# A feed-forward block with seven block products per tile pair, and its output product in one pass over all PSUM banks

## The chip, the cores and the metric

The kernel runs on one core of one Trainium2 chip. The metric is device time in microseconds (us). The kernel before was run three times: median 1025.72 us, 1024.86 to 1025.85 us.

## The reference

One layer of a hybrid encoder on 512 tokens of 1024 channels, in fp32: RMSNorm, one combined projection into three token mixers, a gated merge, an output projection with a residual, and then the feed-forward part, which alone is changed here, and a last RMSNorm:

```
h2 = rmsnorm(x, ffn_norm_g)                              # x: [512 tokens, 1024]
gate, up = jnp.split(h2 @ w_ffn_in, 2, axis=-1)          # each [512, 2816]
x = x + (jax.nn.silu(gate) * up) @ w_ffn_out             # [512, 1024]
out = rmsnorm(x, final_norm_g)
```

## The kernel before

**Operands.** Every large product is formed from fp32 operands that are each split into two float32r parts: a high part (a cast, `hi`) and a low part (`lo = raw - hi`). `mm3` (lines 162 to 165) issues three matmuls for one 128-deep slice: high by high, high by low, low by high. A weight tile of 128 by 1024 is loaded by one 512 KB DMA into one of three buffers (tag `w`, `load_raw`), cast on ScalarE and subtracted on VectorE (`parts`, lines 148 to 156) into two buffers of tag `wh` and two of tag `wl`.

**Feed-forward.** 2816 hidden channels are 22 tiles `m` of 128. For a tile, gate and up are each one PSUM bank [128 channels, 512 tokens], a sum over 8 slices of the 1024 input channels: 2 x 8 x 3 = 48 matmuls of 512 columns (lines 1121 to 1126). The first tile is done in two halves of 256 tokens (`ff0`, lines 1097 to 1102), so that its first half can start before the last token tiles are normed. ScalarE takes SiLU, VectorE multiplies by up, and the product is split into parts at once (lines 1127 to 1140). After every second tile, the two new hidden tiles are multiplied by the first 512 output columns of the output weights, into four banks `acc` (lines 1141 to 1144). When all 22 tiles are done, a second pass over them makes the other 512 output columns (lines 1152 to 1163), token tile after token tile at the end; the last token tile is in two pieces of 256 columns.

**Order.** Instructions are issued by a scheduler that takes them by priority (trace order, with weight loads and their splits raised by `HP`), when a buffer is free in its model. On the chip each engine works its queue in order.

**Around it.** `residual` (line 1080) adds the input to the output projection, norms and transposes a token tile; `norm_B` (line 226) moves it from PSUM into the parts `h2`. The last loop (lines 1159 to 1176) does residual, RMSNorm and the store. V, A, G, T stand for VectorE, ScalarE, GpSimd and TensorE; `cs(k)` is the k-th slice of 128 columns, `U`, `DD`, `TT`, `XT_` take buffers of the pools `up`, `dp`, `tp`, `xp`.

Of the kernel before, what the change touches and what calls it, by code (L numbers as in the profile page):

```python
# [44 lines left out]
# estimated delays of the chains' steps, for the order in which they are traced  # L45
# [10 lines left out]
def trunk(ctx, tc, a, out, dbg=None):  # L56
# [105 lines left out]
    def mm3(ps, lh, ll, rh, rl, first, last):  # L162
        T.matmul(ps, lh, rh, start=first, stop=False)  # L163
        T.matmul(ps, lh, rl, start=False, stop=False)  # L164
        T.matmul(ps, ll, rh, start=False, stop=last)  # L165
# [34 lines left out]
    def rms_factor(xs, ss=None, eng=None):  # L200
        """xs: the halves of a token tile."""
# [887 lines left out]
    ff0 = []  # L1089
    for t in range(NT):  # L1090
# [12 lines left out]
    tap("x2", x2[0][0])  # L1103

# [1 line left out]
    acc = [SM("acc") for _ in range(NT)]  # L1106
    fw = {}
    hid = []

    def ffn_out(k, t, n, ps, c=slice(0, 512)):  # L1110
        if (k // 2, n) not in fw:
            src = a["wfo"][2 * (k // 2):2 * (k // 2) + 2, :, 512 * n:512 * n + 512].rearrange("k p c -> p k c")
            fw[k // 2, n] = load_w(src)
        wh, wl = fw[k // 2, n]
        hh, hl = hid[k]
        r = slice(512 * (k % 2) + c.start, 512 * (k % 2) + c.stop)
        mm3(ps[:, c], hh[:, cs(t)], hl[:, cs(t)], wh[:, r], wl[:, r], k == 0, k == FT - 1)

    for m in range(FT):
        pr = ff0 if m == 0 else []  # L1120
        for g in range(2 if m else 0):
            wh, wl = load_w(a["wfi"][2 * m + g])
            ps = BIG("ff")
            for k in range(KT):
                mm3(ps, wh[:, cs(k)], wl[:, cs(k)], h2.hi(k), h2.lo(k), k == 0, k == KT - 1)
            pr.append(ps)
        s = TT("silu")
        last = A.activation(s, pr[0], AF.Silu)
        V.tensor_tensor(s, s, pr[1], op=ALU.mult)  # L1129
        if m < 4:  # L1130
            ho = op.tile([P, 2, S], F32R, tag="o", name=nm("ho"))
            hh, hl = ho[:, 0], ho[:, 1]
        elif m < 8:
            tg = ("toe", "pt", "sc", "kq")[m - 4]
            hh, hl = XT_("hh", tg, F32R), XT_("hl", tg, F32R)
        else:
            hh, hl = (DD if m < 8 + ND else UU)("hh", F32R)
        A.copy(hh, s)
        V.tensor_tensor(hl, s, hh.bitcast(F32), op=ALU.subtract)
        hid.append((hh, hl))  # L1140
        if m % 2 == 1:
            for k in (m - 1, m):
                for t in range(NT):
                    ffn_out(k, t, 0, acc[t])
# [7 lines left out]
    KF = 18
    pieces = [[(slice(0, 512), BIG("acc2"))] for _ in range(NT - 1)]
    pieces.append([(slice(0, 256), SM("acc2")), (slice(256, 512), SM("acc2"))])
    for k in range(KF):
        for t in range(NT):
            for r, ps in pieces[t]:
                ffn_out(k, t, 1, ps, r)
    for t in range(NT):
        xt, xg = x2[t], TT("xg")  # L1160
        for i, (r, ps) in enumerate(pieces[t]):
            for k in range(KF, FT):
                ffn_out(k, t, 1, ps, r)
            V.tensor_tensor(xt[1][:, r], ps[:, r], xt[1][:, r], op=ALU.add)
            if i < len(pieces[t]) - 1:
                sq_sum(xt[1][:, r], ss[t][:, 1:2])
                V.tensor_tensor(ss[t][:, 0:1], ss[t][:, 0:1], ss[t][:, 1:2], op=ALU.add)
            (V if t == NT - 1 else G).tensor_tensor(xg[:, r], xt[1][:, r], gb[:, 512 + r.start:512 + r.stop], op=ALU.mult)
        G.tensor_tensor(xt[0], xt[0], gb[:, 0:512], op=ALU.mult)  # L1169
        rs = rms_factor([None, xt[1][:, r]], ss[t])  # L1170
        for n, y in enumerate((xt[0], xg)):
            if n == 0 and t < NT - 1:
# [6 lines left out]
def pack(i):  # L1179
    """Lays the inputs out for the loads; no arithmetic."""  # L1180
# [84 lines left out]
```

## Time and profile before

| | |
|---|---|
| three runs | 1025.85, 1025.72, 1024.86 us (median 1025.72) |
| profiled execution | span 1025.0 us from first to last instruction; no other time of it is given |
| TensorE | busy 1005.8 us (98%), 5388 matmuls |
| VectorE / ScalarE / GpSimd | busy 529.8 (52%) / 443.4 (43%) / 139.3 us (14%) |
| feed-forward part | from about 655 us to the end |

Busy time of TensorE overlaps from one matmul to the next, since matmuls are pipelined: what a matmul takes in a dense stream is the distance from its start to the start of the next one. An engine's other instructions are read by their mean duration. In the slices of the page each digit is a fortieth of the span in tenths.

### The profile page before, as it was taken

Reading aid. Unit: us, or ns where it says so; the run is one execution under the profiler, and the core shown is the slowest. Engines: PE = TensorE matmul, PEld = TensorE weight load, DVE = VectorE, ACT = ScalarE, POOL = GpSimd, SP = SyncE. Lnnn points to the kernel's source line nnn. Section 1 sums busy time; section 2 is a strip of 40 time slices with the busy share of each in tenths; the row PEclk is TensorE's granted clock in tenths of the full one; section 3 lists DMA queues with packets and bytes.
Section 4 is the critical chain, followed back from the end, with each engine's and each line's share of the span. In section 5 each row is a group of like instructions: output and inputs, shape, how many; then the busy total and the mean of one; then the engine's idle time right before and its main releaser. Section 6 shows DMA issues by size and latency. Waiting matters only on the chain.

```text
span 1025.0 us, 13638 instructions
## 1 busy us (share of the span) xinstructions
PE 1005.8 (98%) x5388; PEld 820.6 (80%) x5388; DVE 529.8 (52%) x924; ACT 443.4 (43%) x715; POOL 139.3 (14%) x153
## 2 busy tenths in 40 slices
PE   6999999999999999999999999999999999999996
PEld 5777887887887877777888878988888888888885
DVE  6688845486456677766543545633333333233324
ACT  5366345254554557564453644432222222223313
POOL 5115120000223312232121220000000000000201
PEclk8999998699999999999999999999999999999998
DMA  6424271011332211122223235133223322332322
GB/s 213 166 82 123 81 207 62 22 42 63 92 103 83 82 63 62 63 83 83 74 91 103 82 103 185 63 103 103 100 85 103 103 92 94 103 101 85 103 95 90
DMA packets 33008, 98.31 MB, mean 96 GB/s; under 512 B 3504, under 2 KB 3776, under 8 KB 32944
## 3 DMA queue, kind: packets, MB, share of 16 engines
q1 hardware_dynamic: 31120, 91.14, 26.9%
q0 software_dynamic: 1824, 6.31, 2.2%
q8 instruction: 42, 0.69, 0.3%
q14 instruction: 22, 0.18, 0.1%
HBM read 91.65 MB, written 5.78 MB: 95 GB/s over the span
## 4 chain that ended last, share of the span: by engine, by line
PE 94%; DVE 3%; ACT 1%; issue 1%; DMA 1%; POOL 0%; SPq 0%; DVEq 0%; ACTq 0%; POOLq 0%
PE pj L163 11%; PE pj L165 10%; PE pj L164 10%; PE ff L165 8%; PE ff L164 8%; PE ff L163 8%; PE acc L164 4%; PE acc L163 4%; PE acc L165 4%; PE br L163 2%; PE br L165 2%; PE br L164 2%; PE ov L822 1%; PE pv L163 1%; PE pv L165 1%; PE pv L164 1%
## 5 line engine op out<-in xcount | busy, mean ns | idle before, releaser
L151 ACT CAST wh<-w 128x1024 fp32r<-128x1024 f32 x150 | 157.9, 1053 | 406.0 <-PE ff L164 163.9
L155 DVE TENSOR_TENSOR wl<-w,wh 128x1024 fp32r<-128x1024 f32 x148 | 193.9, 1310 | 258.9 <-ACT wh L151 256.4
L163 PE MATMUL pj<-hTh,wh 128*128 128x512 f32 x464 | 185.5, 400 | 0.6 <-DVE cvo L384 0.6
L165 PE MATMUL pj<-hTh,wl 128*128 128x512 f32 x464 | 185.0, 399 | 0.0
L164 PE MATMUL pj<-hTl,wh 128*128 128x512 f32 x464 | 184.6, 398 | 0.0
L163 PE MATMUL ff<-h2h,wh 128*128 128x512 f32 (+1 forms) x368 | 139.9, 380 | 0.0
L165 PE MATMUL ff<-h2h,wl 128*128 128x512 f32 (+1 forms) x368 | 139.8, 380 | 0.0
L164 PE MATMUL ff<-h2l,wh 128*128 128x512 f32 (+1 forms) x368 | 139.8, 380 | 0.0
L163 PEld LDWEIGHTS pj<-hTh,wh 128*128 128x128 f32 x464 | 87.8, 189 | 19.9 <-issue 2.2
L165 PEld LDWEIGHTS pj<-hTh,wl 128*128 128x128 f32 x464 | 88.0, 190 | 18.9 <-issue 1.6
L164 PEld LDWEIGHTS pj<-hTl,wh 128*128 128x128 f32 x464 | 88.0, 190 | 18.2 <-issue 1.3
L164 PEld LDWEIGHTS ff<-h2l,wh 128*128 128x128 f32 x368 | 69.2, 188 | 13.2
L163 PEld LDWEIGHTS ff<-h2h,wh 128*128 128x128 f32 x368 | 69.2, 188 | 13.1
L165 PEld LDWEIGHTS ff<-h2h,wl 128*128 128x128 f32 x368 | 69.2, 188 | 13.0
L164 PE MATMUL acc<-wl,hh 128*128 128x512 f32 (+1 forms) x162 | 59.5, 367 | 0.0
L163 PE MATMUL acc<-wh,hh 128*128 128x512 f32 (+1 forms) x162 | 59.2, 366 | 0.0
L1169 POOL TENSOR_TENSOR x<-x,gb 128x512 f32<-128x512 f32 x4 | 6.0, 1540 | 343.6 <-ACT sq L195 343.6
L1129 DVE TENSOR_TENSOR silu<-silu,ff 128x512 f32<-128x512 f32 x22 | 15.1, 688 | 72.2 <-PE ff L165 72.2
L165 PE MATMUL acc<-wh,hh 128*128 128x512 f32 (+1 forms) x126 | 46.0, 365 | 0.0
L163 PE MATMUL br<-oh,wh 128*128 128x512 f32 x96 | 38.2, 398 | 0.0
L165 PE MATMUL br<-oh,wl 128*128 128x512 f32 x96 | 37.7, 392 | 0.0
L1029 POOL TENSOR_TENSOR y<-y,yt 128x512 f32<-128x512 f32 x16 | 22.5, 1406 | 110.6 <-DVE yt L1028 110.6
(319 smaller groups left out, 1602.2 us busy)
## 6 DMA issues: line engine op xcount, KB each, us to landing
w<-in_wb SPq DMA_DIRECT2D x60, 512.0 KB, 3.5
w<-in_wfi SPq DMA_DIRECT2D x44, 512.0 KB, 3.5
w<-in_wfo SPq DMA_DIRECT2D x22, 512.0 KB, 3.5
w<-in_wbr SPq DMA_DIRECT2D x12, 512.0 KB, 3.5
w<-in_wv SPq DMA_DIRECT2D x8, 512.0 KB, 3.6
w<-in_wout SPq DMA_DIRECT2D x8, 512.0 KB, 3.5
x<-in_x SPq DMA_DIRECT2D x4, 512.0 KB, 7.2
toe<-in_toe SPq DMA_DIRECT2D x8, 256.0 KB, 2.9
```

Of the source, the lines that this page charges most:

```text
L151: A.copy(hi, raw)
L155: (eng or V).tensor_tensor(lo, raw, hi.bitcast(F32), op=ALU.subtract)
L163: T.matmul(ps, lh, rh, start=first, stop=False)
L164: T.matmul(ps, lh, rl, start=False, stop=False)
L165: T.matmul(ps, ll, rh, start=False, stop=last)
L822: T.matmul(po[64 * hh:64 * hh + 64, 0:P], av[kt][:, h * 64:(h + 1) * 64], PT[hh][:, cs(kt)], start=kt == 0, stop=kt == qb, tile_position=( ...
L1029: G.tensor_tensor(y[m], y[m], t, op=ALU.add)
L1129: V.tensor_tensor(s, s, pr[1], op=ALU.mult)
L1169: G.tensor_tensor(xt[0], xt[0], gb[:, 0:512], op=ALU.mult)
```

## The change

- Gate rows and up rows of a hidden tile form a block row pair, the two halves of the 1024 input channels a block column pair, and the two halves of the tokens the columns of the other factor. The 2x2 by 2x2 block product is done with seven block products instead of eight (for tiles 1 to 21; tile 0 stays as it was). One block product is 4 slices x 3 matmuls of 256 columns.
- Four sums of input blocks (`x11`, `x12`, `x22`, `x21`) are formed once from an fp32 copy `xf` of the normed tokens that `norm_B` writes besides, three on V and one on G, and split into parts. For each tile, four sums of weight blocks are formed on G, and seven weight blocks of 128 by 512 are split into parts (A casts, V subtracts), in nine rotating buffers.
- The products land in three PSUM banks of 256 columns, the three of `pb` for even tiles and three of `pq` for odd ones; A and V combine them into gate and up. Some products are added onto a bank that was read in between.
- The hidden tiles are kept in fp32 and split when the output product needs them. That product comes after all tiles: all 1024 output columns and four token tiles in eight banks at once, slice by slice for 19 of the 22, then token tile by token tile for the last three.

```diff
-    def norm_B(r, t, o):
+    def norm_B(r, t, o, xf):
...
             V.tensor_tensor(o.l[n][:, :, sl], ph, o.h[n][:, :, sl].bitcast(F32), op=ALU.subtract)
+            A.copy(xf[n][t // 2][:, :, (t % 2) * P:(t % 2) * P + P], ph)
...
+    xf = [[op.tile([P, 4, 256], F32, tag="o", name=nm("xf")) for _ in range(2)] for _ in range(2)]
...
+    def split(src, hi, lo):
+        A.copy(hi, src)
+        V.tensor_tensor(lo, src, hi.bitcast(F32), op=ALU.subtract)
+        return hi, lo
+
+    with tc.high_priority(offset=HP):
+        (x11, x12), (x21, x22) = xf
+        V.tensor_tensor(x11, x12, x11, op=ALU.subtract)
+        G.tensor_tensor(x12, x22, x12, op=ALU.subtract)
+        V.tensor_tensor(x22, x22, x11, op=ALU.subtract)
...
+        T2 = tparts(x22, "T2")
+        V.tensor_tensor(x21, x21, x22, op=ALU.subtract)
+        T3 = tparts(x12, "T3")
+        T1 = tparts(x11, "T1")
+        T4 = split(x21, h2.h[0][:, :, RH], h2.l[0][:, :, RH])
+    B11, B21, B22 = [(h2.h[j][:, :, r], h2.l[j][:, :, r]) for j, r in ((0, LH), (1, LH), (1, RH))]
...
+        c = ("wh", "wl", "d", "o", "wh", "wl", "d", "o", "o")[slot[0] % 9]
...
+    def ffn_weights(m):
+        with tc.high_priority(offset=HP):
+            (a11, a12), (a21, a22) = [halves(load_raw(a["wfi"][2 * m + g])) for g in range(2)]
+            s1, s2, s3, s4 = [XT_("s", c) for c in ("toe", "pt", "sc", "kq")]
+            r = {1: split(a11, *slot2())}
+            G.tensor_tensor(s1, a21, a22, op=ALU.add)
+            G.tensor_tensor(s2, s1, a11, op=ALU.subtract)
+            r[6] = split(s2, *slot2())
+            G.tensor_tensor(s3, a11, a21, op=ALU.subtract)
+            r[7] = split(s3, *slot2())
+            r[2] = split(a12, *slot2())
+            r[5] = split(s1, *slot2())
+            r[4] = split(a22, *slot2())
+            G.tensor_tensor(s4, a12, s2, op=ALU.subtract)
+            r[3] = split(s4, *slot2())
+        return r
+
+    def ffn_pair(m, h):
+        w = ffn_weights(m)
+        mk = SM if m % 2 else BIG
+        pa, pm, pg = [mk("ff")[:, LH] for _ in range(3)]
...
+            for k in range(4):
+                mm3(ps, w[i][0][:, cs(k)], w[i][1][:, cs(k)], b[0][:, k], b[1][:, k], first and k == 0, k == 3,
+                    not first)
+
+        product(1, pa, B11, True)
+        A.copy(c1, pa)
+        product(6, pm, T2, True)
+        V.tensor_tensor(u2, pm, c1, op=ALU.add)
+        product(7, pg, T3, True)
+        V.tensor_tensor(u3, pg, c1, op=ALU.add)
+        product(2, pa, B21, False)
+        A.activation(g1, pa, AF.Silu)
+        product(5, pm, T1, False)
+        V.tensor_tensor(u3, pm, u3, op=ALU.add)
+        product(4, pg, T4, False)
+        V.tensor_tensor(u2, pg, u2, op=ALU.add)
+        V.tensor_tensor(h[:, LH], g1, u2, op=ALU.mult)
+        product(3, pm, B22, False)
+        V.tensor_tensor(c1, pm, c1, op=ALU.add)
+        last = A.activation(c1, c1, AF.Silu)
+        V.tensor_tensor(h[:, RH], c1, u3, op=ALU.mult)
...
+    acc = {tn: (BIG if i < 3 else SM)("acc") for i, tn in enumerate(order)}
+    KF = 19
...
+    def out_weights(k):
+        with tc.high_priority(offset=HP):
+            if k % 3 < 2:
+                w = [wp.tile([P, D], F32R, tag=c, name=nm(c), bufs=2) for c in ("wh", "wl")]
+            else:
+                w = [op.tile([P, D], F32R, tag="o", name=nm("wo")) for _ in range(2)]
+            fw[k] = DD("hh", F32R), w
+            split(load_raw(a["wfo"][k]), *w)
+            split(hid[k], *fw[k][0])
...
+    for k in range(KF):
+        out_weights(k)
+        for t, n in order:
+            ffn_out(k, t, n)
+    for k in range(KF, FT):
+        out_weights(k)
     gb = bc_row(2)
     for t in range(NT):
+        xt, xg, ss = x2[t], [XT_("xg", c) for c in ("toe", "pt")], rms_rows()
+        for n in range(2):
             for k in range(KF, FT):
+                ffn_out(k, t, n)
+            V.tensor_tensor(xt[n], acc[t, n], xt[n], op=ALU.add)
+            sq_sum(xt[n], ss[:, n:n + 1])
+            (V if t == NT - 1 and n == 1 else G).tensor_tensor(xg[n], xt[n], halves(gb)[n], op=ALU.mult)
+        rs = rms_scale(ss)
...
```

The weights, their number of bytes and all that stands ahead of `residual` are the same.

## Rows read from the trace of the kernel before

**Rows 1.** The page: busy time, share of the span and instructions of each engine.
```profile
PE 1005.8 (98%) x5388; PEld 820.6 (80%) x5388; DVE 529.8 (52%) x924; ACT 443.4 (43%) x715; POOL 139.3 (14%) x153
```
**Rows 2.** The chain that ended last, by engine.
```profile
PE 94%; DVE 3%; ACT 1%; issue 1%; DMA 1%; POOL 0%; SPq 0%; DVEq 0%; ACTq 0%; POOLq 0%
```
**Rows 3.** Windows by stage: us, then each engine's busy us (instructions), clock, DMA share.
```profile
655.00:667.00 12.00, 11.96 (x100) 11.67 (x100) 5.79 (x11) 5.17 (x10) 0.00 (x0) 1.00 0.13 45
667.00:953.00 286.00, 286.00 (x1264) 236.87 (x1264) 93.30 (x97) 80.64 (x98) 0.00 (x0) 1.00 0.29 98
953.00:1005.00 52.00, 52.00 (x278) 44.83 (x278) 14.59 (x13) 12.09 (x17) 6.04 (x4) 1.00 0.28 92
```
**Rows 4.** Waits within 680 to 950 us: total, times, longest.
```profile
ACT wh L151 <- PE ff L164: 153.1, 39, 4.1
DVE wl L155 <- ACT wh L151: 114.8, 30, 3.9
```
**Rows 5.** Timeline, TensorE: start, duration; 512-column and 256-column matmuls side by side.
```profile
984.70 0.39 PE L163 MATMUL acc<-wh,hh 128*128 128x512 f32 x1
984.93 0.39 PE L164 MATMUL acc<-wl,hh 128*128 128x512 f32 x1
985.16 0.39 PE L165 MATMUL acc<-wh,hh 128*128 128x512 f32 x1
985.38 0.28 PE L163 MATMUL acc<-wh,hh 128*128 128x256 f32 x1
```
**Rows 6.** Timeline, TensorE: first and last of 65 256-column matmuls in a row.
```profile
659.41 0.28 PE L164 MATMUL ff<-h2l,wh 128*128 128x256 f32 x1
...
667.08 0.28 PE L165 MATMUL ff<-h2h,wl 128*128 128x256 f32 x1
```
**Rows 7.** Groups by form: busy us, mean ns of one, idle before.
```profile
L1139 DVE TENSOR_TENSOR hh<-silu,hh 128x512 fp32r<-128x512 f32 x14 | 9.6, 685 | 0.0
L1164 DVE TENSOR_TENSOR x<-acc,x 128x256 f32<-128x256 f32 x2 | 0.8, 418 | 0.0
L1138 ACT CAST hh<-silu 128x512 fp32r<-128x512 f32 x18 | 11.2, 624 | 0.0
L151 ACT CAST wh<-w 128x1024 fp32r<-128x1024 f32 x150 | 157.9, 1053 | 406.0 <-PE ff L164 163.9 <-PE pj L164 131.9 <-PE acc L165 76.7
L815 ACT COPY PT<-pT 128x256 f32<-128x256 f32 x8 | 3.0, 372 | 4.4 <-PE pT L813 4.3
L195 ACT ACTIVATE sq<-x 128x256 f32<-128x256 f32 x2 | 0.8, 417 | 0.9 <-DVE x L1164 0.9
L155 POOL TENSOR_TENSOR wl<-w,wh 128x1024 fp32r<-128x1024 f32 x2 | 5.0, 2512 | 4.1 <-ACT wh L151 4.1
```
**Rows 8.** Timeline, GpSimd and VectorE near 537 us.
```profile
536.79 1.29 POOL L1029 TENSOR_TENSOR y<-y,yt 128x512 f32<-128x512 f32 x1 [1.43 <-DVE yt L1028]
536.88 2.28 DVE L155 TENSOR_TENSOR wl<-w,wh 128x1024 fp32r<-128x1024 f32 x1 [0.17 <-ACT wh L151]
```
**Rows 9.** Timeline, GpSimd and VectorE from 955.7 to 960.1 us.
```profile
955.74 0.69 DVE L1150 TENSOR_TENSOR x<-acc,x 128x512 f32<-128x512 f32 x1
956.54 1.30 POOL L1169 TENSOR_TENSOR x<-x,gb 128x512 f32<-128x512 f32 x1
956.87 2.05 DVE L155 TENSOR_TENSOR wl<-w,wh 128x1024 fp32r<-128x1024 f32 x1 [0.44 <-ACT wh L151]
957.79 2.28 POOL L1169 TENSOR_TENSOR x<-x,gb 128x512 f32<-128x512 f32 x1
```
**Rows 10.** Timeline, VectorE at 79 us, and GpSimd beside it.
```profile
79.18 4.01 DVE L155 TENSOR_TENSOR wl<-w,wh 128x1024 fp32r<-128x1024 f32 x1
...
81.06 1.04 POOL L588 TENSOR_TENSOR Es<-Es,bb 128x512 f32<-128x512 f32 x1
```
**Rows 11.** DMA issues: KB each, median us from issue to landing.
```profile
w<-in_wfi SPq DMA_DIRECT2D x44, 512.0 KB, 3.5
```
**Rows 12.** Timeline: the norm of the last token tile, and a split of tile 1.
```profile
658.82 1.25 ACT L229 CAST h2h<-nT 128x512 fp32r<-128x512 f32 x2 [2.00 <-PE nT L222]
659.44 1.36 DVE L230 TENSOR_TENSOR h2l<-nT,h2h 128x512 fp32r<-128x512 f32 x2 [0.70 <-ACT h2h L229]
665.48 1.23 DVE L155 TENSOR_TENSOR wl<-w,wh 128x1024 fp32r<-128x1024 f32 x1 [4.67 <-ACT wh L151]
```
**Rows 13.** Timeline, the end: last matmul, and VectorE's last steps.
```profile
1016.66 0.28 PE L165 MATMUL acc<-wh,hh 128*128 128x256 f32 x1
...
1018.21 0.42 DVE L1164 TENSOR_TENSOR x<-acc,x 128x256 f32<-128x256 f32 x1
1019.40 0.21 DVE L207 TENSOR_SCALAR ss<-ss 128x1 f32<-128x1 f32 x1
```

More of the change, by code (lines that the diff above doesn't have):

```diff
@@ L160, in load_w, with mm3 @@
             return parts(load_raw(src, n), n)
[L162 to L165, printed above, removed]
+    def mm3(ps, lh, ll, rh, rl, first, last, goes_on=False):
+        T.matmul(ps, lh, rh, start=first, stop=False, skip_group_check=goes_on)
+        T.matmul(ps, lh, rl, start=False, stop=False, skip_group_check=goes_on)
+        T.matmul(ps, ll, rh, start=False, stop=last, skip_group_check=goes_on)
     def preload(after):
@@ L205, in rms_factor, with rms_scale @@
         sq_sum(xs[1], ss[:, 1:2], eng)
+        return rms_scale(ss)
+    def rms_scale(ss):
         y, v, t = ss[:, 1:2], ss[:, 2:3], ss[:, 3:4]
@@ L1094, in trunk @@
         if t > 0:
-            norm_B(residual(t - 1), t - 1, h2)
-    norm_B(residual(NT - 1), NT - 1, h2)
+            norm_B(residual(t - 1), t - 1, h2, xf)
+    norm_B(residual(NT - 1), NT - 1, h2, xf)
+    LH, RH = slice(0, 256), slice(256, 512)
     ff0 = [BIG("ff") for _ in range(2)]
-    for half in range(2):
-        r = slice(256 * half, 256 * half + 256)
+    for r in (LH, RH):
         for g, (wh, wl) in enumerate(w0):
@@ L1103, in trunk @@
     tap("x2", x2[0][0])
-    acc = [SM("acc") for _ in range(NT)]
-    fw = {}
[L1108 to L1144, printed above, removed]
@@ L1145, in trunk, with tparts @@
-    preload(last)
+    s0 = TT("silu")
+    A.activation(s0, ff0[0], AF.Silu)
+    hid = [U("hid")]
+    V.tensor_tensor(hid[0], s0, ff0[1], op=ALU.mult)
+    def split(src, hi, lo):
[7 more added lines that the diff above has]
+        V.tensor_tensor(x22, x22, x11, op=ALU.subtract)
+        def tparts(src, s):
+            return split(src, *[dp.tile([P, 4, 256], F32R, tag="d", name=nm(s + c)) for c in "hl"])
+        T2 = tparts(x22, "T2")
[3 more added lines that the diff above has]
+        T4 = split(x21, h2.h[0][:, :, RH], h2.l[0][:, :, RH])
@@ new lines, in trunk, with slot2 @@
+    B11, B21, B22 = [(h2.h[j][:, :, r], h2.l[j][:, :, r]) for j, r in ((0, LH), (1, LH), (1, RH))]
+    slot = [0]
+    def slot2():
+        c = ("wh", "wl", "d", "o", "wh", "wl", "d", "o", "o")[slot[0] % 9]
+        slot[0] += 1
+        if c in "do":
+            t = (dp if c == "d" else op).tile([P, 2, 512], F32R, tag=c, name=nm("wq"))
+        else:
+            t = wp.tile([P, 2, 512], F32R, tag=c, name=nm("wq"), bufs=2)
+        return t[:, 0], t[:, 1]
+    def ffn_weights(m):
[14 more added lines that the diff above has]
+        return r
@@ new lines, in ffn_pair, with product @@
+    def ffn_pair(m, h):
+        w = ffn_weights(m)
+        mk = SM if m % 2 else BIG
+        pa, pm, pg = [mk("ff")[:, LH] for _ in range(3)]
+        e1, e2 = TT("e1"), TT("e2")
+        c1, u2, u3, g1 = e1[:, LH], e1[:, RH], e2[:, LH], e2[:, RH]
+        def product(i, ps, b, first):
+            for k in range(4):
[18 more added lines that the diff above has]
+        V.tensor_tensor(h[:, RH], c1, u3, op=ALU.mult)
+        hid.append(h)
+        return last
@@ new lines, in trunk @@
+    h2x = None
+    for m in range(1, FT):
+        if m < FT - 2:
+            h = U("hid")
+        else:
+            if h2x is None:
+                h2x = op.tile([P, 2, 512], F32, tag="o", name=nm("hid"))
+            h = h2x[:, m - FT + 2]
+        last = ffn_pair(m, h)
+    preload(last)
+    acc = {tn: (BIG if i < 3 else SM)("acc") for i, tn in enumerate(order)}
+    KF = 19
+    fw = {}
+    def out_weights(k):
+        with tc.high_priority(offset=HP):
+            if k % 3 < 2:
+                w = [wp.tile([P, D], F32R, tag=c, name=nm(c), bufs=2) for c in ("wh", "wl")]
+            else:
+                w = [op.tile([P, D], F32R, tag="o", name=nm("wo")) for _ in range(2)]
+            fw[k] = DD("hh", F32R), w
+            split(load_raw(a["wfo"][k]), *w)
+            split(hid[k], *fw[k][0])
@@ L1146, in trunk, with ffn_out @@
+    def ffn_out(k, t, n):
+        (hh, hl), (wh, wl) = fw[k]
+        mm3(acc[t, n], hh[:, cs(t)], hl[:, cs(t)], halves(wh)[n], halves(wl)[n], k == 0, k == FT - 1)
+    for k in range(KF):
[4 more added lines that the diff above has]
+        out_weights(k)
     gb = bc_row(2)
-    ss = [rms_rows() for _ in range(NT)]
     for t in range(NT):
-        V.tensor_tensor(x2[t][0], acc[t], x2[t][0], op=ALU.add)
-        sq_sum(x2[t][0], ss[t][:, 0:1])
@@ L1152, in trunk @@
[L1152 to L1161, printed above, removed]
-            for k in range(KF, FT):
[L1163 to L1172, printed above, removed]
+        xt, xg, ss = x2[t], [XT_("xg", c) for c in ("toe", "pt")], rms_rows()
@@ L1173, in trunk @@
+        for n in range(2):
+            for k in range(KF, FT):
+                ffn_out(k, t, n)
[3 more added lines that the diff above has]
+        rs = rms_scale(ss)
+        for n, y in enumerate(xg):
+            if n == 0:
                 A.activation(y, y, AF.Copy, scale=rs)
```

1 line of the change is left out of this document (removed).

## The prediction

> **What bounds the kernel now.** I read the page's busy times first: TensorE is busy 98% of the span, every other engine at most half [rows 1]. The chain of waits says the same, 94% of it is TensorE [rows 2]. Then windows by stage: from 667 to 1005 us TensorE has no idle time at all, at the full clock of 2.4 GHz (granted 1.00), while VectorE works 93.3 and ScalarE 80.6 of 286 us and GpSimd nothing [rows 3]. The table of waits shows which way the waiting goes: the splits of the weights wait for TensorE to give a buffer back, up to 4.1 us each, never the reverse [rows 4]. So before, this stage is paid by its matmuls alone, and the preparation has slack. Two questions decide: how much matmul time goes, and whether the preparation, which more than doubles per tile, still fits under what is left.
>
> **The matmuls.** In a dense stream a 512-column matmul starts 0.2267 us after the last one (984.70 to 985.38 for three) [rows 5], a 256-column one 0.1198 us (7.67 us for 64 steps) [rows 6]. A hidden tile is 48 x 0.2267 = 10.88 us before, and 7 x 12 = 84 matmuls of 256 columns after, 84 x 0.1198 = 10.06 us (1.44 us a product). That is 0.82 us less, not an eighth: 256 columns cost 53% of 512. Over 21 tiles: -17.2 us. The 132 output matmuls of 256 columns become 66 of 512: 15.81 - 14.96 = -0.85 us.
> The Trainium skill (TensorE: Matmul & The Clock Gate, Back-to-back issue gap) gives N/2.4 + 2.5 ns at the full clock. By that rule a tile would go from 10.36 to 9.17 us and 21 tiles would give 25 us. The rows just named are some 11 ns longer per matmul at either width, and they decide.
>
> **What a tile now asks of the other engines.** ScalarE: seven casts of 0.624, two activations or copies out of PSUM of about 0.37 and one of 0.417 [rows 7]: 5.5 us of 10.06, hidden. VectorE: seven subtractions of 0.685, and seven 256-column steps of 0.418 (five read PSUM, two are SiLU times up with both inputs in SBUF) [rows 7]: 4.80 + 2.93 = 7.7 us. GpSimd: four sums of 128x512 at 1.29 [rows 8]: 5.2 us. Each alone fits. But VectorE and GpSimd don't run side by side on such work: a split of 128x1024 that takes 1.23 alone [rows 12] takes 2.28 when it starts 0.09 us behind a GpSimd sum, ending 1.08 after it [rows 8]. The other way round, a GpSimd product issued during VectorE's split ends 1.15 us after that (960.07 against 958.92) [rows 9]. A step that reads PSUM is untouched: 0.69 beside GpSimd [rows 9]. So one that waited holds the other up for less than its full duration: 1.15 us for a GpSimd sum, and 0.55 for a 512-column subtraction (1.08 less 512 columns' worth, 0.53).
> The Trainium skill (SBUF — State Buffer, Who interferes with whom) says that a VectorE instruction with two SBUF inputs and a GpSimd instruction that reads SBUF exclude each other, and that the second waits until the first has finished. The trace agrees (2.28 against 1.23). It speaks against this change, which puts 5.2 us of GpSimd sums beside 5.6 us of such VectorE work per tile; priced at full durations, that is rival 3 below.
>
> **The period of a tile** is then the longest of three rings:
> - TensorE: 10.06 us.
> - VectorE: 7.7 us of its own, and per GpSimd sum 1.15 less what VectorE does meanwhile out of PSUM (0.42 at best, one step) less the 0.13 that its waiting step saves: 0.60 to 1.02. Four of them: 7.7 + 2.4 = 10.1 to 7.7 + 4.1 = 11.8 us.
> - GpSimd: the two weight tiles of a hidden tile lie in two of three buffers, and both are read until its last sum (`s4`) or nearly so. The next tile's second weight tile is loaded only then, and the next `s1` needs it. So: load 3.5 us to landing [rows 11] with 0.2 for the semaphores, `s1` 1.29 and half a subtraction ahead of it (0.3), then three sums that each let one waiting subtraction through, 3 x (0.55 + 1.15) = 5.1. Together 10.4 us; if nothing stands in the way, 3.7 + 5.2 = 8.9; if each waits for a full 0.685 and takes 1.29, 3.7 + 7.9 = 11.6.
> I take 10.4, the longest of the three at the durations the rows show. The nine buffers let preparation run about eight products ahead of TensorE, so a late subtraction by itself stalls nothing; a period over 10.06 does, every tile: 20 x 0.34 = +6.8 us for tiles 2 to 21.
>
> **Once only.** (a) The start. `x11` to `T4` come behind the last token tile's norm, whose low parts end at 660.8 [rows 12]; the extra copies put the fp32 copy at 661.4. From there VectorE must do, before product 3 of tile 1: three sums of 1.23 and a wait behind GpSimd's `x12` (2.51, from the 128x1024 form [rows 7]), four low parts of 1.23, tile 0's multiplication 0.69, five of the seven weight subtractions 3.4, five steps of 0.42: 17.3 us, so to 678.7. TensorE would be there at 667.2 + 6 x 1.44 = 675.8. That is 2.9 us late, and 5.3 if the four sums of tile 2 fall into it too (4 x 0.6); I take 4.1, bounds 0 (the order hides it) to 8. (b) Two more ScalarE copies per token tile, about 0.6 each [rows 12]: the last norm comes 0.6 to 1.1 later, against a left half of tile 0 that ends about as the norm does now. 0 to 1.1, I take 0.5. (c) The last split. The weight buffers of slice 21 come free when slice 18 ends; a cast and a subtraction of 128x1024 need about 2.4 us and cover is seven matmuls, 1.6 us. The same place exists before, so 0 to 0.8; I take 0.5. (d) The end. Now VectorE takes up the last sum 1.55 us after the last matmul started (1018.21 against 1016.66), being still at the token tile before, and the end is 8.3 us after it [rows 13]. After, token tiles are 18 matmuls or 4.1 us apart and the last add follows within 0.3: 1.25 gained, but add and square are 512 wide in place of 256 (0.27 + 0.21 more). -0.8 us. Splits of hidden tiles and output weights during the output product (VectorE 1.23 + 0.69, ScalarE 1.05 + 0.62 us per slice [rows 7, 12]) lie under 24 x 0.2267 = 5.4 us of matmuls and cost nothing; DMA bytes are the same.
>
> **The sum**, on the profiled span of 1024.95 us (the median of the runs is 0.8 above it): -17.2 - 0.85 + 6.8 + 4.1 + 0.5 + 0.5 - 0.8 = -7.0, so 1018.0, and 1018.8 as a median. It changes sign at a period of 10.75 us: (1025.7 - 1012.0) / 20 above 10.06.
>
> **Rivals.** (1) *TensorE stays the bound.* Period 10.06 to 10.25, about 1012. For it: VectorE's ring has 10.1 as its low end, and the slot order may give the next load the buffer that is free after `s3`. Against: three rings within 4% of each other seldom all run at their best. (2) *VectorE becomes the bound, slower.* Its queue is in order; if two steps with SBUF inputs stand behind a GpSimd sum instead of one that reads PSUM, VectorE idles 1.0 and not 0.6 us per sum. Period 11.0 at the middle, 1031; 11.8 at worst, 1047. The product that shows it first is 3, which writes the bank that VectorE must have read since product 5, with one product (1.44 us) between. It decides from 10.75 on, that is, when two of three sums meet no PSUM step. For it: the subtraction and the PSUM step of a product are both released by the same end of a product, so their order is fragile. Against: before, GpSimd and VectorE take turns [rows 9]. (3) *Full durations.* If neither engine saves anything by waiting, 5.2 + 4.8 + 0.84 = 10.8 us must pass one after the other: 1026.8, no change. The short ends of waited steps (1.08, 1.15) speak against it. (4) *VectorE is starved or the queues stand in the wrong order*, so that the seven products don't run dense at all: one split took 4.01 us while GpSimd went through two sums and a select [rows 10]. With no overlap at all, 7.7 + 5.2 = 12.9 a tile, 1069.
>
> **Chances.** My forecast (period 10.25 to 10.65, 1016 to 1024) 0.32; rival 1 0.15; rival 3 and what lies around break-even 0.13; rival 2 0.33; rival 4 0.07. Faster and slower count from 0.2%, 2 us, which is what can be told from no change: faster 0.47, same 0.13, slower 0.40. The range leaves out 1 in 10 on either side: below, rival 1 with a free start, 1009; above, most of rival 2, 1044.
>
> **What would show it.** Starts of 256-column matmuls 0.120 us apart within a product (if not, the first term falls). Tile starts 10.4 us apart from tile 3 on; gaps of TensorE ahead of weight loads released by VectorE or ScalarE splits, which wait for GpSimd, which waits for the DMA, would bear out the GpSimd ring. Gaps ahead of product 3 released by an add on PSUM would mean rival 2. GpSimd sums of 1.29 to 1.9 and subtractions up to 1.7 us long show the turns. One gap of some 4 us near 670 us is the start. A VectorE busy time in the stage near 10 us a tile with GpSimd's waits for DMA absent would make the forecast wrong.

## The result, and the profile after

The changed kernel took 1062.03 us (median of 4 runs, 1060.66 to 1065.70), the kernel before 1025.53 us beside it: a ratio of 1.0366, 95% interval 1.0347 to 1.0386. It is 3.7% slower; 1019 with a range of 1009 to 1044 was predicted. The profiled execution has a span of 1058.9 us, 33.9 more than before.

The page of the changed kernel, busy times and the granted clock in 40 slices. [Rows 1] had TensorE at 98% for fewer matmuls:

```profile
PE 1004.6 (95%) x6078; PEld 852.5 (81%) x6078; DVE 658.3 (62%) x1158; ACT 501.0 (47%) x873; POOL 262.7 (25%) x238
PEclk9999997899999999999999999999899988999999
```

Matmul time (1004.6) is as before, though each hidden tile has less of it, and the clock's digits fall to 8 in the last third. A busy share names the cause of neither. The chain of waits, [rows 2] before 94% TensorE, now breaks off inside the changed stage after a fifth of the span, so its shares don't say either:

```profile
PE 15%; DVE 1%; POOL 1%; issue 1%; DMA 1%; ACT 1%; DVEq 0%; POOLq 0%; ACTq 0%; SPq 0%
```

Its earliest steps do give a hint (start, duration): from 854 to 871 us it runs from a low part (a subtraction on VectorE) to a load of weights, to GpSimd's sums, to the next load (after L1157 come L1158 and L1165).

```profile
855.26 0.61 DVE wq L1120
855.93 3.45 DMA w<-in_wfi
859.52 1.28 POOL s L1157
...
865.73 3.37 DMA w<-in_wfi
```

So by windows: the norm of the last tokens, the 21 tiles of seven products, the output product. Columns as in [rows 3].

```profile
655.00:667.00 12.00, 11.88 (x100) 11.68 (x99) 7.40 (x13) 5.90 (x13) 2.43 (x2) 1.00 0.15 45
667.00:931.00 264.00, 230.72 (x1771) 226.93 (x1770) 196.59 (x307) 115.95 (x224) 116.28 (x80) 0.94 0.28 89
931.00:1050.00 119.00, 119.00 (x527) 98.19 (x525) 42.57 (x58) 36.67 (x56) 7.75 (x6) 1.00 0.28 89
```

The first and the last are full, at the whole clock. The middle one is where the time is: from the first product at 667.14 to the last at 930.87 us it lasts 263.7 us, and 21 x 10.06 = 211.3 were to be had. The clock there is 0.94. All gaps of TensorE between two matmuls of the stage add up to some 37 us; and for 34.1 us the granted clock was 0.5 (1.2 GHz), where 256-column matmuls start 0.213 us apart in place of 0.120: by estimate 34.1 x (1 - 0.120 / 0.213) = 14.9 us. Together 52, which is the whole excess.

The waits from 667 to 931 us (engine, line and tile, what it waited for, us in total, times, longest):

```profile
POOL s L1157 <- DMA w<-in_wfi: 120.9, 19, 13.3
DVE wq L1120 <- ACT wq L1119: 52.2, 49, 5.5
ACT wq L1119 <- PE ff L166: 49.7, 47, 3.4
ACT wq L1119 <- POOL s L1158: 44.2, 15, 6.7
...
PE ff L164 <- DVE e L1190: 15.5, 5, 5.4
...
PE ff L164 <- ACT e L1182: 12.2, 5, 2.9
```

[Rows 4] had only preparation waiting for TensorE. Here TensorE waits too, and the table read from below gives the order: TensorE waits for an add (L1190) or a copy (L1182) out of PSUM; ScalarE's casts (L1119) wait for GpSimd's sum `s2` (L1158); GpSimd's first sum `s1` (L1157) waits for the load of weights, 19 times of 21.

The groups of these lines, by form:

```profile
L1120 DVE TENSOR_TENSOR wq<-s,wq 128x512 fp32r<-128x512 f32 x84 | 80.0, 953 | 45.2 <-ACT wq L1119 44.2
L1157 POOL TENSOR_TENSOR s<-w 128x512 f32<-128x512 f32 x21 | 29.2, 1392 | 142.7 <-DMA w<-in_wfi 120.9 <-DVE ss L216 12.3 <-DVE e L1186 9.6
L1158 POOL TENSOR_TENSOR s<-s,w 128x512 f32<-128x512 f32 x21 | 31.5, 1499 | 0.1
```

Beside [rows 7] (685) and [rows 8] (1.29), the subtraction is 953 ns on the mean and a sum 1392 to 1504 (the lines of `s1` and `s2` are shown): they do take turns. But they are not what is short of time; GpSimd stands idle for 142.7 us ahead of `s1`.

One stall in full: the timeline of GpSimd, ScalarE, VectorE and TensorE from 753 to 769 us, and the request of a load on SyncE's queue (start, duration; in brackets the idle time ahead of the instruction and what ended it). L1165 is `s4`, L1160 `s3`, L1120 the low parts, L1188 a SiLU out of PSUM.

```profile
753.58 1.29 POOL L1165 TENSOR_TENSOR s<-w,s 128x512 f32<-128x512 f32 x1
758.67 1.29 POOL L1157 TENSOR_TENSOR s<-w 128x512 f32<-128x512 f32 x1 [3.80 <-DMA w<-in_wfi]
759.92 1.26 POOL L1160 TENSOR_TENSOR s<-w,w 128x512 f32<-128x512 f32 x1
761.14 1.26 POOL L1158 TENSOR_TENSOR s<-s,w 128x512 f32<-128x512 f32 x1
...
754.90 0.33 SPq L116 DMA_DIRECT2D w<-in_wfi  x1
...
762.43 0.62 ACT L1119 CAST wq<-s 128x512 fp32r<-128x512 f32 x1 [6.67 <-POOL s L1158]
...
768.25 0.62 ACT L1119 CAST wq<-w 128x512 fp32r<-128x512 f32 x1 [3.37 <-PE ff L166]
...
763.08 1.21 DVE L1120 TENSOR_TENSOR wq<-s,wq 128x512 fp32r<-128x512 f32 x1 [5.46 <-ACT wq L1119]
764.22 0.68 DVE L1120 TENSOR_TENSOR wq<-w,wq 128x512 fp32r<-128x512 f32 x1
764.82 0.41 DVE L1190 TENSOR_TENSOR e<-ff,e 128x256 f32<-128x256 f32 x1
...
768.90 0.69 DVE L1120 TENSOR_TENSOR wq<-w,wq 128x512 fp32r<-128x512 f32 x1 [0.23 <-ACT wq L1119]
...
759.60 0.28 PE L166 MATMUL ff<-h2h,wq 128*128 128x256 f32 x1
765.28 0.58 PE L164 MATMUL ff<-h2h,wq 128*128 128x256 f32 x1 [5.40 <-DVE e L1190]
765.66 0.42 PE L165 MATMUL ff<-h2l,wq 128*128 128x256 f32 x1
765.88 0.41 PE L166 MATMUL ff<-h2h,wq 128*128 128x256 f32 x1
```

The weights that `s1` waits for were requested at 754.90 us, 0.03 after `s4` ended, and landed 3.6 later. `s3` and `s2` follow, and only then the cast of `s2`, which stands at the head of ScalarE's queue and has waited 6.67 us. Its low part is at the head of VectorE's queue, and the add L1190, whose input, product 5, TensorE had finished by 758.5, is two places behind it. Product 3 needs that add. TensorE stands still for 5.40 us, for a part of the weights that belongs to the tile after the next; the queues have it ahead of two parts of the next. When it goes on, matmuls start 0.21 apart, no longer 0.12. The next request is later still after its `s4`: it comes at 769.66, behind the low part of 768.90, whose cast waited 3.37 us for TensorE to leave a part buffer.

The end: the last matmul and VectorE's steps behind it, as in [rows 13].

```profile
1050.00 0.39 PE L166 MATMUL acc<-wh,hh 128*128 128x512 f32 x1
...
1050.66 1.33 DVE L1251 TENSOR_SCALAR xg<-xg,ss 128x512 f32<-128x512 f32 x1
1051.92 0.68 DVE L1243 TENSOR_TENSOR x<-acc,x 128x512 f32<-128x512 f32 x1
```

### The profile page after: what moved, and what is told of

The parts are those of the page before. It is cut to its first block, busy times and chain, and to the rows that moved or that the text cites. A ratio compares the mean times of both kernels' runs of the same rounds, so it can differ in the third digit from the quotient of the medians.

```text
span 1058.9 us, 15666 instructions
## 1 busy us (share of the span) xinstructions
PE 1004.6 (95%) x6078; PEld 852.5 (81%) x6078; DVE 658.3 (62%) x1158; ACT 501.0 (47%) x873; POOL 262.7 (25%) x238
## 5 line engine op out<-in xcount | busy, mean ns | idle before, releaser
L155 DVE TENSOR_TENSOR wl<-w,wh 128x1024 fp32r<-128x1024 f32 x84 | 114.7, 1366 | 96.0 <-ACT wh L151 95.7
L151 ACT CAST wh<-w 128x1024 fp32r<-128x1024 f32 x86 | 90.2, 1049 | 159.5 <-PE pj L165 131.7
L164 PE MATMUL ff<-h2h,wq 128*128 128x256 f32 x336 | 100.6, 299 | 27.8 <-DVE e L1190 15.5
L1120 DVE TENSOR_TENSOR wq<-s,wq 128x512 fp32r<-128x512 f32 x84 | 80.0, 953 | 45.2 <-ACT wq L1119 44.2
L166 PE MATMUL ff<-h2h,wq 128*128 128x256 f32 x336 | 98.6, 294 | 0.6 <-DVE wq L1120 0.6
L165 PE MATMUL ff<-h2l,wq 128*128 128x256 f32 x336 | 99.0, 295 | 0.0
L1119 ACT CAST wq<-s 128x512 fp32r<-128x512 f32 x84 | 51.4, 617 | 95.2 <-POOL s L1158 44.2
L164 PEld LDWEIGHTS ff<-h2h,wq 128*128 128x128 f32 x336 | 68.6, 204 | 30.2 <-DVE e L1190 16.5
L166 PEld LDWEIGHTS ff<-h2h,wq 128*128 128x128 f32 x336 | 68.3, 204 | 0.8 <-DVE wq L1120 0.8
L165 PEld LDWEIGHTS ff<-h2l,wq 128*128 128x128 f32 x336 | 68.6, 204 | 0.0
L1157 POOL TENSOR_TENSOR s<-w 128x512 f32<-128x512 f32 x21 | 29.2, 1392 | 142.7 <-DMA w<-in_wfi 120.9
L1120 DVE TENSOR_TENSOR wq<-w,wq 128x512 fp32r<-128x512 f32 x63 | 51.4, 818 | 8.3 <-ACT wq L1119 8.0
L1119 ACT CAST wq<-w 128x512 fp32r<-128x512 f32 x63 | 38.7, 618 | 35.5 <-PE ff L166 23.4
L1120 DVE TENSOR_TENSOR wl<-w,wh 128x1024 fp32r<-128x1024 f32 x15 | 18.4, 1225 | 56.3 <-ACT wh L1119 55.8
```

Source lines behind the costliest of these rows:

```text
L151: A.copy(hi, raw)
L155: (eng or V).tensor_tensor(lo, raw, hi.bitcast(F32), op=ALU.subtract)
L164: T.matmul(ps, lh, rh, start=first, stop=False, skip_group_check=goes_on)
L165: T.matmul(ps, lh, rl, start=False, stop=False, skip_group_check=goes_on)
L166: T.matmul(ps, ll, rh, start=False, stop=last, skip_group_check=goes_on)
L1119: A.copy(hi, src)
```

## The experiments

Two theories at first (the expectations tell them in full). **L**: the ring through the load sets the period of a tile: the load of the next tile's second weight tile waits for the last reader of a raw buffer, then come landing, `s1`, `s3`, `s2`, a cast and low parts, which free the next buffer. **P**: the turns that VectorE and GpSimd take are enough for 12 us a tile by themselves. To compare stages I use one window, 722 to 875 us, in which all of these kernels run nothing but tiles of seven products: 153 us x 84 matmuls / the count of matmuls is the period. The row of the changed kernel gives 153 x 84 / 1021 = 12.6 us:

```profile
722.00:875.00 153.00, 131.70 (x1021) 129.85 (x1019) 106.49 (x168) 60.39 (x121) 74.68 (x52) 0.94 0.27 86
```

| kernel | median us | ratio to before, 95% | period in the window |
|---|---|---|---|
| changed kernel | 1062.03 | 1.0366 [1.0347, 1.0386] | 12.6 |
| out_only | 1024.23 | 0.9982 [0.9963, 1.0002] | |
| one_load | 1028.92 | 1.0039 [1.0024, 1.0054] | 10.5 |
| raw4 | 1034.82 | 1.0092 [1.0077, 1.0107] | 10.8 |
| sums_v | 1025.08 | 0.9995 [0.9982, 1.0008] | 10.2 |
| raw4_sums_v | 1027.73 | 1.0031 [1.0022, 1.0041] | 10.3 |
| tile1_old | 1012.54 | 0.9876 [0.9860, 0.9893] | 10.3 |
| tile1_old_raw4 | 1021.20 | 0.9953 [0.9932, 0.9974] | 10.4 |
| tile1_old_gsums | 1061.22 | 1.0357 [1.0337, 1.0376] | 12.6 |
| raw_first | 1058.97 | 1.0313 [1.0267, 1.0359] | 11.9 |
| tile1_old_nu28 | 1012.37 | 0.9883 [0.9866, 0.9899] | 10.2 |
| slots11 | 1052.02 | 1.0281 [1.0227, 1.0335] | 11.8 |
| tile1_old_slots11 | 1013.82 | 0.9903 [0.9873, 0.9932] | 10.4 |

**out_only**: the one-pass output product alone, with gate and up as before (eight block products; no copies `xf`, no block sums).

```diff
     def ffn_pair(m, h):
-        w = ffn_weights(m)
-        mk = SM if m % 2 else BIG
...
+        pr = []
+        for g in range(2):
+            wh, wl = load_w(a["wfi"][2 * m + g])
+            ps = BIG("ff")
+            for k in range(KT):
+                mm3(ps, wh[:, cs(k)], wl[:, cs(k)], h2.hi(k), h2.lo(k), k == 0, k == KT - 1)
+            pr.append(ps)
...
```

> Gate and up as before the change (eight block products, 48 matmuls of 512 columns), output product in one pass over eight banks as in the changed kernel. Both theories: the output product is not the cause, 1024 to 1028 us, tile period 10.9 us. If the one pass costs what was lost: over 1040 us.

1024.23 us, no change. The output product in one pass costs nothing, and the whole loss is in the seven products and what is prepared for them.

**one_load**: the raw weights are loaded once and used for all 21 tiles, so the loads of tiles 2 to 21 are left out.

```diff
+    kept = []
...
+            if not kept:
+                kept.extend(load_raw(a["wfi"][2 * m + g]) for g in range(2))
-            (a11, a12), (a21, a22) = [halves(load_raw(a["wfi"][2 * m + g])) for g in range(2)]
+            (a11, a12), (a21, a22) = [halves(w) for w in kept]
```

> Leaves out the loads of the gate and up weights of tiles 2 to 21 (all tiles use those of tile 1), so no sum waits for a load. Theory L (load ring: the second weight tile is loaded only when the last split out of its buffer is done, the sums wait for it, and in-order ScalarE and VectorE queues hold PSUM steps behind the splits of sums): tile period falls from 12.0 to 10.1 to 10.8 us, the time from 1062 to 1025 to 1038 us. Theory P (the turns that VectorE and GpSimd take at the SBUF are enough for 12 us): period stays at 11.7 to 12.0, time 1055 to 1062 us.

1028.92. With the same sums, splits and matmuls the stage falls from 263.7 to 230.9 us. Windows of one_load:

```profile
722.00:875.00 153.00, 149.44 (x1229) 147.68 (x1228) 146.98 (x206) 74.63 (x146) 80.56 (x56) 1.00 0.00 1
```

The load is in the ring: P alone gives 10.5 us, not 12. VectorE is busy 146.98 of 153 there (its subtractions last 1022 to 1063 ns on the mean beside GpSimd's sums), so this is about what the turns cost.

**raw4**: a fourth raw weight buffer, for one buffer of tag `up` less.

```diff
-NU, ND, NTMP = 29, 8, 6
+NU, ND, NTMP = 28, 8, 6
-        raw = wp.tile([P, n], F32, tag="w", name=nm("w"))
+        raw = wp.tile([P, n], F32, tag="w", name=nm("w"), bufs=4)
```

(and so for the other use of tag `w`, in `bc_row`)

> A fourth buffer for raw weights (and one of 29 small buffers less, to make room). The next tile's second weight tile can be loaded while this one is still read. Theory L: as without loads, 1025 to 1040 us, and GpSimd's waits for the load go from 121 us to under 40. Theory P: 1055 to 1062 us.

1034.82, with all loads. Taking the wait of the load for the last reader out of the ring does nearly what taking the load out did. It points to L again. GpSimd's waits for the load fall from 120.9 us to 67.6 in the stage and not under 40 as expected, but preparation has a lead again: ScalarE's casts wait for TensorE (62.2 us in the window, 75 times).

**sums_v**: the four sums of weight blocks on VectorE; GpSimd does nothing in the stage.

```diff
-            G.tensor_tensor(s1, a21, a22, op=ALU.add)
+            V.tensor_tensor(s1, a21, a22, op=ALU.add)
```

(and so for `s2`, `s3`, `s4`)

> The four weight sums per tile on VectorE, three raw buffers as in the changed kernel. No turns are taken with GpSimd; VectorE has 7.7 + 4 x 0.69 = 10.5 us of its own per tile. Theory P: period 10.5, 1030 us. Theory L: the ring is shorter too (four sums in 2.8 us), but the sums still wait for the load, now at the head of VectorE's queue: period 10.8 to 11.5, 1036 to 1052 us.

1025.08, and a period of 10.2, under what either theory gave. Its ring, mean of tiles 3 to 19: 3.74 from the request of the load to the start of `s1`, 3.78 to the end of `s4`, 2.57 to the next request, 10.1 in all; in the changed kernel 3.69 + 5.84 + 2.67 = 12.2. VectorE with four more instructions a tile is faster than the two engines side by side. The 10.1 is TensorE's own pace: ScalarE's casts wait for TensorE here (63.3 us in the window, 76 times), so the ring by itself may be shorter still. What is left of the loss is ahead of tile 4: about 9 us of gaps and 10.2 us at half the clock before 704 us.

**raw4_sums_v**: both.

> Both cuts at once: four raw buffers and the sums on VectorE. Theory L (the load closes the ring; each cut opens it): little is left to win over one cut, period 10.1 to 10.3 us from tile 4 on, 1020 to 1025 us. Theory P (turns and VectorE's own load set the pace): as with the sums on VectorE alone, 10.3 us or more, 1024 to 1028 us. What is left over TensorE's 10.06 us after this is the start of the stage under both.

1027.73: not faster than sums_v. It lies outside what L gave and inside what P gave, but tells little between them: with the ring at 10.1 us TensorE is the longest already, and GpSimd has no sums to take turns with. The start is no better (gaps of 17 us in the stage, one of 3.79 at 683.98).

**tile1_old**: sums_v, `x12` on VectorE too, and tile 1 in the old form with 48 matmuls, which gives the block sums of the tokens 10.9 us more.

```diff
+    ff1 = [SM("ff") for _ in range(2)]
+    for g in range(2):
+        wh, wl = load_w(a["wfi"][2 + g])
+        for k in range(KT):
+            mm3(ff1[g], wh[:, cs(k)], wl[:, cs(k)], h2.hi(k), h2.lo(k), k == 0, k == KT - 1)
...
-        G.tensor_tensor(x12, x22, x12, op=ALU.subtract)
+        V.tensor_tensor(x12, x22, x12, op=ALU.subtract)
...
-    for m in range(1, FT):
+    for m in range(2, FT):
```

> Sums on VectorE, the input sum x12 too, and tile 1 done the old way (48 matmuls of 512 columns, 10.9 us in place of 10.06), so that the input sums and their parts are made under it. If the start of the stage (gaps of some 9 us and 10 us at 1.2 GHz between 665 and 704 us in the run with the sums on VectorE) is what is left: 1012 to 1018 us, faster than before, no gap over 1 us. If the gaps only move to tile 2: 1022 to 1026 us.

1012.54: faster than both kernels, 1.2% under before. One gap of over 1 us is left (1.45 at 818). Windows and waits (722 to 875 us) of tile1_old; L1128 is the cast here, L1166 `s1`, now on VectorE:

```profile
722.00:875.00 153.00, 151.05 (x1248) 149.88 (x1248) 135.24 (x265) 75.32 (x146) 0.00 (x0) 1.00 0.32 101
```
```profile
ACT wq L1128 <- PE ff L166: 62.4, 72, 2.1
...
DVE s L1166 <- DMA w<-in_wfi: 3.2, 7, 1.7
```

Preparation waits for TensorE again, as in [rows 4], and of the waits for the load 3.2 us are left.

**tile1_old_raw4** and **tile1_old_nu28**: tile1_old with the fourth raw buffer, and with only the buffer of tag `up` taken away.

> As tile1_old, with four raw buffers. Theory L and P both: the same within 4 us, 1009 to 1016 us; a larger gain would mean that the load still closes a ring with the sums on VectorE.

> tile1_old with 28 buffers of tag up in place of 29, and three raw weight buffers. It tells whether tile1_old_raw4 lost its 8.7 us by the fourth raw buffer or by the buffer of tag up given for it. If by the buffer of up: 1019 to 1023 us. If by the fourth raw buffer (loads earlier, another order): 1011 to 1015 us.

1021.20 and 1012.37. The first is a miss, and the second says that it is the fourth raw buffer itself that costs 8.7 us where the sums are on VectorE. In the profiled run it is one gap of TensorE behind the matmul of 686.32, and 6.8 us at half the clock that go with it. The trace of tile1_old_raw4 tells what ends the gap (L1116 is tile 0's multiplication of SiLU by up, which reads PSUM; L1167 is a sum, `s2`):

```profile
689.41 0.68 DVE L1167 TENSOR_TENSOR s<-s,w 128x512 f32<-128x512 f32 x1
690.01 0.68 DVE L1116 TENSOR_TENSOR hid<-silu,ff 128x512 f32<-128x512 f32 x1
...
690.84 0.55 PE L164 MATMUL ff<-h2h,wq 128*128 128x256 f32 x1 [4.24 <-DVE hid L1116]
```

It is the order of VectorE's queue again. With a fourth raw buffer, sums and low parts of later tiles stand ahead of tile 0's multiplication, which starts at 690.0 here, at 667.3 in tile1_old and at 666.8 in tile1_old_nu28. The fourth buffer moves it back in the other pairs too: from 668.1 (sums_v) to 681.8 (raw4_sums_v), and from 677.4 (changed kernel) to 684.4 (raw4). One of the ten runs of tile1_old_raw4 took 1011.05 us; it has no trace, so whether the gap was missing there is not known.

**tile1_old_gsums**: tile1_old with the four sums back on GpSimd.

> tile1_old with the four sums of each hidden tile back on GpSimd, so the changed kernel with only its start mended. Theory L (the ring load, sums, splits sets the period of every hidden tile): tile starts some 12.0 us apart from tile 3 on, as in the changed kernel, against 10.5 in tile1_old: 1012.5 + 20 x 1.5 = 1043 us, bounds 1035 to 1050, and gaps of TensorE with the clock at half after them go on through the whole stage. Rival S (the late start throws the stage off, and it never comes back into step): with a start in time the sums cost GpSimd what they cost in the kernel with one load, period 10.4 to 10.6, 1010 to 1018 us.

1061.22. A start in time gains nothing while the ring is long: the period is 12.6, and S falls. It is over the 1050 that was the upper end of L, which reckoned 12.0 a tile; the clock is 0.91 in the window.

**raw_first**: the splits of the raw halves ahead of the splits of the sums.

```diff
             G.tensor_tensor(s2, s1, a11, op=ALU.subtract)
-            r[6] = split(s2, *slot2())
+            r[2] = split(a12, *slot2())
+            r[4] = split(a22, *slot2())
             G.tensor_tensor(s3, a11, a21, op=ALU.subtract)
+            G.tensor_tensor(s4, a12, s2, op=ALU.subtract)
+            r[6] = split(s2, *slot2())
...
```

> The changed kernel with the same work, in another order within a tile: the splits of the two raw halves (products 2 and 4) ahead of the splits of the sums, so that the last reader of the raw buffers is GpSimd's sum s4 and no longer a subtraction of VectorE. Theory L, in the form that it is the last split out of the raw buffer that holds the next load back: the load is issued within 0.2 us of s4's end in place of 2.4 us on the mean, the period falls from 12.0 to about 10 to 10.6, and the time to 1025 to 1035 us. If the ring is long because four sums and the subtractions between them take turns, wherever the last split stands: period 11.5 to 12.2, 1050 to 1066 us.

1058.97, the second of the two forecasts (one of its four runs took 1049.05). But the edit did not do what it was to do: the scheduler still put a split of a sum second in the queues, splits of raw halves then waited for part buffers, and from the end of `s4` to the next request it is 2.40 us on the mean of tiles 3 to 19, against 2.67 in the changed kernel. So it tells nothing on where the last reader stands. No run here moves the last reader alone; its place is read from timelines, and what the wait for it costs is shown by raw4.

**slots11**: eleven buffers for the split parts in place of nine.

```diff
-        c = ("wh", "wl", "d", "o", "wh", "wl", "d", "o", "o")[slot[0] % 9]
+        c = ("wh", "wl", "d", "o", "wh", "wl", "d", "o", "o", "o", "o")[slot[0] % 11]
```

(with five buffers of tag `o` in place of four, 28 of `up` in place of 29)

> The changed kernel with eleven buffers for the split weight parts in place of nine (tag o has one that the rotation of nine leaves idle, one more is made from a buffer of tag up); GpSimd's sums, three raw buffers and the order of the work stay. In the changed kernel the ring of a tile is 12.2 us on the mean of tiles 3 to 19: load to first sum 3.69, first to end of last sum 5.84, and 2.67 from there to the next load. Theory L with this addition (L+): the 2.67 are splits of the raw halves that wait, at the head of ScalarE's queue, for TensorE to leave one of the nine part buffers; two more give them two products (2.9 us) of lead, the load follows the last sum by 0 to 1 us, the period falls to 10.3 to 11.0 and the time to 1027 to 1042 us. If the splits stand late for other reasons (the queue's order behind the PSUM steps): the delay stays 2 to 3 us, 1055 to 1066 us.

1052.02, between the two forecasts. L+ is wrong in its point: in the window, ScalarE's casts waited for TensorE 27 times in the changed kernel, 26.7 us in all, and here that wait does not occur; yet the delay from `s4` to the next request is 2.80 us on the mean. What the two buffers did is to make every tile alike, and that lays the ring bare. Windows, then the timeline of GpSimd, ScalarE, VectorE and TensorE from 771.5 to 785.5 us, with two requests of loads on SyncE's queue:

```profile
722.00:875.00 153.00, 134.16 (x1092) 131.52 (x1091) 98.12 (x182) 62.47 (x130) 66.81 (x53) 1.00 0.30 90
```
```profile
779.63 1.37 POOL L1157 TENSOR_TENSOR s<-w 128x512 f32<-128x512 f32 x1 [6.47 <-DMA w<-in_wfi]
780.95 1.30 POOL L1160 TENSOR_TENSOR s<-w,w 128x512 f32<-128x512 f32 x1
782.21 1.30 POOL L1158 TENSOR_TENSOR s<-s,w 128x512 f32<-128x512 f32 x1
783.59 1.30 POOL L1165 TENSOR_TENSOR s<-w,s 128x512 f32<-128x512 f32 x1
...
776.09 0.33 SPq L116 DMA_DIRECT2D w<-in_wfi  x1
...
787.83 0.33 SPq L116 DMA_DIRECT2D w<-in_wfi  x1
...
772.46 1.24 DVE L1120 TENSOR_TENSOR wq<-s,wq 128x512 fp32r<-128x512 f32 x1 [3.88 <-ACT wq L1119]
773.62 0.41 DVE L1192 TENSOR_TENSOR e<-ff,e 128x256 f32<-128x256 f32 x1
774.07 0.42 DVE L1193 TENSOR_TENSOR hid<-e,e 128x256 f32<-128x256 f32 x1
774.41 0.68 DVE L1120 TENSOR_TENSOR wq<-s,wq 128x512 fp32r<-128x512 f32 x1
775.01 0.42 DVE L1195 TENSOR_TENSOR e<-ff,e 128x256 f32<-128x256 f32 x1
775.35 0.68 DVE L1120 TENSOR_TENSOR wq<-w,wq 128x512 fp32r<-128x512 f32 x1
...
784.19 1.24 DVE L1120 TENSOR_TENSOR wq<-s,wq 128x512 fp32r<-128x512 f32 x1 [3.88 <-ACT wq L1119]
...
776.71 0.39 PE L164 MATMUL ff<-h2h,wq 128*128 128x256 f32 x1 [1.39 <-ACT e L1182]
```

Read it from 776.09, when the load is requested, to 787.83, the next request, 11.74 us: 3.54 to `s1`; 3.88 through `s1`, `s3`, `s2` (to 783.51); and 4.32 from there: the cast of `s2`, its low part at 784.19 (1.24 beside `s4`), two steps of the running tile, the low part of `s3`, a step, and the low part of `a12`, which is the last to read the raw buffer. The low parts of one tile earlier show these last five steps, 773.62 to 776.03, with the request at 776.09 right behind. VectorE waits 3.88 us in each round, so it is not the bound; the order of its queue is. TensorE waits 1.39 us a tile for the copy L1182, which stands behind the same steps.

**tile1_old_slots11**: tile1_old with eleven part buffers.

> tile1_old (sums on VectorE, old form for tile 1) with eleven part buffers. There the ring of a tile is 9.9 us, under TensorE's 10.06, and TensorE has some 4 us of gaps in the stage: 1008 to 1012.5 us by L+ (the rest of the gaps goes), 1011 to 1015 if the part buffers play no part.

1013.82, no gain: with the sums on VectorE nothing waits long for part buffers.

## Why the prediction was wrong

**The matmuls: right.** Within a product of the changed kernel they start 0.12 us apart (758.76, 758.88, 759.00), tiles without a stall are 10.08 us apart, and the output product takes 119.1 us (528 x 0.2267 = 119.7). The stage begins at 667.14 (667.2 foreseen), so the norm copies (b) cost no more than the 0.5 allowed.

**The step that failed is the GpSimd ring**: "both are read until its last sum (`s4`) or nearly so. The next tile's second weight tile is loaded only then", priced at 10.4 us. Its engine, its wait (GpSimd for the DMA, 19 of 21 times) and its load (3.7) were right, and the sums even shorter than taken (5.84 in place of 6.7). The "nearly so" was 2.67 us: the last reader is a low part on VectorE, in slots11 that of `a12`, which stands behind two low parts that wait for `s2` and `s3` and behind three steps of the running tile. In the uniform rounds of slots11 that makes 11.7 us, and 1.7 us over TensorE's 10.06 in each of 20 tiles is 33 us where +6.8 stood. In the changed kernel the ring is 12.2 us (3.69 + 5.84 + 2.67), and from tile 2 on the stage takes 46.6 us more than 20 x 10.06: some 33 of gaps and, by the estimate below, 13.4 by the clock. one_load, raw4 and sums_v each take out or shorten another link, and come to 10.2 to 10.8 us. The sentence beside it, that with nine buffers "a late subtraction by itself stalls nothing", failed too: in the stall of 5.40 us the add that product 3 needs stands behind a late subtraction in VectorE's queue.

**The clock: missing from the sum.** In the changed kernel, with nine part buffers, the delay comes in lumps: nine gaps of 2.3 to 5.6 us. In or behind seven of them and behind those of the start, the granted clock was 0.5 for 3.4 or 6.8 us: 34.1 us, 14.9 us of loss. [Rows 3] showed 1.00 all through, and the prediction let it stand, though it forecast gaps. slots11 has gaps of about 1.5 us, one in each tile (1.39 of wait in its row), and the clock at 1.00 from 722 on. TensorE is idle as long in its stage as in the changed kernel's (33.2 and 33.3 us), but it has 13.7 us at 0.5 in place of 34.1, by the same estimate 8.9 us less lost, and is 10 us faster. The Trainium skill (TensorE: Matmul & The Clock Gate, Part 1: The HAM clock gate) says that "the default state is throttled, and activity releases the throttle"; the rows agree as far as they go: the clock fell only in or behind gaps.

**Rival 2, half right.** The place was foreseen (product 3, released by an add on PSUM, 5 times, and as often product 2 by the copy), and so was the order of VectorE's queue as what makes TensorE wait. But VectorE is not the bound: it is busy 106.49 of 153 us and waits, through a cast and the sums, for a load. Its own work was put too high, at 7.7 us, by adding durations: in the changed kernel low parts in a row start 0.60 apart at 0.69 of duration (673.16, 673.76, 674.36), and the add at 764.82 0.60 behind a subtraction of 0.68. Rival 3 asks for 10.8 us at least; one_load takes 10.5 with the same sums, which speaks against it. Rival 4's 1069 comes nearest to the measured time, and of its two causes the order of the queues holds. Its mechanism, no overlap of VectorE and GpSimd, does not: several tiles run dense at 10.08, and one_load stays at 10.5.

**The Trainium skill's rule on the shared port** (SBUF — State Buffer, Who interferes with whom) is that the two engines exclude each other on such work. The rows agree that it costs: 1.24 beside a sum, 685 ns in sums_v. By one_load it brings the period to 10.5 us, about break-even; the other 1.2 to 2 us need the load.

**The start (a)**: tile 2 starts 16.07 us after tile 1 where 10.06 would do, so 6.0 in place of 4.1, inside its bounds. Mended alone it gains nothing (tile1_old_gsums); with a short ring it gains 12.5 us (tile1_old against sums_v), about what sums_v lost there by gaps (9) and by the clock (10.2 us at half speed, 4.5).

**The end (d)**: 8.9 us after the last matmul and not 7.5. The last add is taken up 1.92 us after the last matmul started, since VectorE is still scaling the token tile before (1.33), which the prediction had out of the way.

## What to carry to other kernels

When work moves onto more engines, write down who is the last reader of each buffer that a load waits for, and what stands ahead of that reader in its queue: a ring is priced along the queues, not by the engines' busy times. A helper engine that shortens another's list can lengthen the ring; here VectorE alone (10.1 us, TensorE's own pace) beat VectorE with GpSimd (12.2). And more buffers can make it worse: they let work for later tiles into a queue ahead of a step that TensorE waits for now (tile1_old_raw4). A forecast of gaps on TensorE has to price what the clock does after them as well.

## What was not expected of the hardware

The clock of TensorE fell to 0.5 within a kernel that is busy 95% of its span: after the gap of 5.40 us the next matmuls start 0.21 us apart, and the window from 766 to 772 us, with TensorE busy throughout, has 0.79. In slots11, with a gap of about 1.5 us in every tile, it stays 1.00 from 722 us on. A subtraction on VectorE that lasts 0.69 lets the next start after 0.60 (673.16, 673.76, 674.36 us), so sums over durations overstate a full queue of them by some 15%.
